# A list scheduler's model of TensorE in the input stage of a pooling and recurrence layer: waits for splits, x operands and a bank's last sum, and a rank penalty

## The chip, the cores and the metric

The kernel runs on one core of one Trainium2 chip. The metric is the device time of one execution in microseconds (us). The time of the kernel before is the median of three runs.

## The reference

One layer of a decoder, in fp32, for 2048 new tokens and 8 sequences of 8 tokens that go on from a state. Cut to what matters:

```python
xn = rms_norm(x, norm_pre)
z = einsum('btd,de->bte', xn, w_in)          # D 1024 -> 4096: v_pool, g_pool, u_lru, g_lru
y_pool = pool_mixer(v_pool, ...)             # windows 2/4/8/16 minus the token, a 256x256 map per group, a scale
xs = causal_conv(u_lru, ...)                 # depthwise, width 4
y_lru = rg_lru(xs, ...)                      # gates r, i = sigmoid(xs @ w + b), h = a*h + u along the tokens
mixed = concat([y_pool * silu(g_pool), y_lru * silu(g_lru)])
out = x + rms_norm(einsum('bte,ed->btd', mixed, w_out), norm_post)
```

The last rows of the pool and conv inputs and the recurrence's last state are outputs too.

## The kernel before

**Numbers and products.** TensorE multiplies fp32 operands that are split in two parts, a high one (rounded by ACT) and a low one (the rest, subtracted by DVE); three matmuls (high by high, high by low, low by high) stand for one. The input product z = xn @ w_in is tiled in three macros (m = 0, 1, 2) of 704 tokens each and in 16 quads of output channels, V (pool input), G (pool gate), U (recurrence input) and L (recurrence gate) by p = 0 to 3. In macro 0 a quad is eight plain half products. In macros 1 and 2 it is one level of Strassen-Winograd: seven products of 12 matmuls each, numbered 1 to 7 (`pid`), which are summed in three PSUM banks named a, e and d with macro and kind (a1G is bank a of a G quad in macro 1). Products 1, 6, 7 and 4 go through bank a, 5 and 3 through e, 2 through d. When a product is done, an evacuation copies the bank (ACT, L1011) or adds it to the result (DVE, L1007), and a later product of the same bank starts with what the earlier one left only after that evacuation has read it.

**Operands.** The x operands of the seven products are X11, X22, X21 and the sums T1 to T4 of quarters of x. They lie in one buffer, XN, that all quads of a macro share. At the change of macro, `transition` (L1340 to 1391) makes them anew: a raw sum on DVE (`x_raw`), the high part on ACT (`x_hi`, L334 and L336) and the low part on DVE (`x_lo`, L321). T2's sum needs T1's, T4's needs T2's. The weights' parts are loaded raw in macro 0 and for the last quads of macro 1, summed and split there (`w1V` from `wr1V`, `hi_lo` at L843), and stored in a DRAM scratch `wsd`, from where the other quads load them ready-made (`w2V<-wsd`, `w_step` at L897) six products ahead (AHEAD).

**Around the products.** Each finished quad starts a chain of work: the cumulative sums and differences of the pool and its map (six matmuls, bank y), the convolution and the two gates (six matmuls each, banks r and i, operands xh and xl), the gates' activations, the scan along the tokens, and SiLU. The row norms of the next macro are computed too (`tok_rsqrt`, L291 to 299: five small DVE operations with a square root on ACT between). After the input stage comes the output product, seven products by the same scheme with banks p.

**What sets the order.** Each engine runs its instructions in the order in which the program issues them. In the input stage that order is made in Python, on the host, by a list scheduler with a model of time: `T[0]` is the model's time, `clock` holds when DVE ("V"), ACT ("A") and GpSimd ("G") will be free. Each chain of work is a generator (a job) that yields the engine it needs next and for how long. `one_slot` (L1462) issues one product (`pe_fn`), then the evacuations of the product before (`run_evacs`, L1449), then at most one gate or map, and then fills the slot: `run_jobs` (L781) grants to jobs what can start before the slot's end, the earliest start first; among starts that are within 0.05 us of each other the lower rank wins. A slot lasts SLOT = 1.94 us and 0.98 for a gate or map, longer if the evacuations end later. Where a product needs something that is not issued yet, `need_w` (L910), `need_x` (L1393) and `need_small` (L954) issue it on the spot; the model's time does not move on for that. `quad_slot` (L1031) issues a product and hands its evacuation to the next slot. If no free buffer is left for the next quad, a later product may be issued ahead; this is how product 4 of a quad comes to stand behind products of the next one, or in front of them.

Of the kernel before, what the change touches and what calls it, by code (L numbers as in the profile page):

```python
# [52 lines left out]
LATE = 544  # L53
N_TT = (T_ALL + P - 1) // P
NBLK = 16
SLOT = 1.94
HOP = 0.2
OVER = 1.0
AHEAD = 6
# [14 lines left out]
def hymba_kernel(  # L74
# [392 lines left out]
    A = {}  # L467
# [268 lines left out]
    w_tiles, w_rawt = {}, {}  # L736
# [44 lines left out]
    def run_jobs(end):  # L781
        moved = True
        while moved:
            moved = False
            for job in list(jobs):
                while job in jobs:
                    e, arg = job["req"][:2]
                    if e == "?" and arg():
                        job["ready"] = max(job["ready"], T[0])
                    elif e == "t":  # L790
                        job["ready"] += arg
                    elif e == "D" and job["ready"] <= end:
                        pass
                    else:
                        break
                    advance(job)
            best = None
            for job in jobs:
                s = fits(job, end)
                if s is None:  # L800
                    continue
                req = job["req"]
                late = s + (TABLE_COST if len(req) > 2 and table[0] not in TABLES[req[2]] else 0.0)
                if best is None or late < best[0] - 0.05:
# [35 lines left out]
    def w_key(kind, p, pid):  # L840
        return wsd[:, (KINDS[kind] // 8 * NG + p) * 7 + pid - 1, :]

    def hi_lo(hi, lo, src, store=None):  # L843
        yield "A", 0.62
        AC.copy(out=hi, in_=src)
        yield "V", 0.71
        tsub(lo, src, hi.bitcast(F32))
        if store:
            yield "t", LAG
            yield "D", 0  # L850
            nc.sync.dma_start(out=w_key(*store[1:]), in_=store[0].bitcast(F32))
# [3 lines left out]
    def plain_tile(q, n):  # L855
        t = w_tiles[q, n] = half_tile(f"w{q[2]}{q[1]}_{n}")
        store = (flat_of(t), q[2], q[1], PLAIN_PID[n]) if n in PLAIN_PID else None
        w_jobs[q, n] = spawn(hi_lo(t[:, 0, :], t[:, 1, :], w_rawt[q, n], store), rank=0)

    def s_sum(q, i):  # L860
        r11, r12, r21, r22 = (w_rawt[q, n] for n in NAMES)
# [31 lines left out]
    def w_step(q, pid):  # L893
        m, p, kind = q
        t = w_tiles[q, pid] = half_tile(f"w{m}{kind}{p}_{pid}")
        if not is_late(q) or pid in (1, 2, 4):
            nc.sync.dma_start(out=flat_of(t).bitcast(F32), in_=w_key(kind, p, pid))  # L897
            return
        n = S_PID.index(pid)
        if n == 0:  # L900
            w_jobs[q, "s"] = {"n": 0, "job": spawn(s_sums(q, lambda i: w_jobs[q, "s"].update(n=i + 1)),
                                                        max(T[0], w_time[q]), rank=0)}
        box = w_jobs[q, "s"]

        def wait_split():
            yield "?", lambda: box["n"] > n
            yield from hi_lo(t[:, 0, :], t[:, 1, :], w_rawt[q, S_OF[pid]], (flat_of(t), kind, p, pid))
        w_jobs[q, pid] = spawn(wait_split(), rank=0)

    def need_w(q, n):  # L910
        if (q, "s") in w_jobs and w_jobs[q, "s"]["n"] < 4 and n in (5, 6, 7, 3):
            job = w_jobs[q, "s"]["job"]
            while w_jobs[q, "s"]["n"] <= S_PID.index(n):
                grant(job, max(clock["V"], job["ready"], T[0]))
        job = w_jobs.pop((q, n), None)
        if job:
            force(job)

    small = {}

# [10 lines left out]
    def load_small(m, kind, p):  # L931
        t = sb.tile([P, 2, 512], F32R, tag=kind, bufs=1, name=f"{kind}{m}_{p}")
        small[kind] = t
        flat = t.rearrange("p a b -> p (a b)").bitcast(F32)
        i = 0 if kind == "pw" else 1
        if m:
            nc.sync.dma_start(out=flat, in_=swd[:, i, p, :])
            return
        if (kind, p) not in small_raw:
            small_early(kind, p)  # L940
        r = small_raw.pop((kind, p))

        def work():
            yield "A", 0.62
            AC.copy(out=t[:, 0, :], in_=r)
            yield "V", 0.71
            tsub(t[:, 1, :], r, t[:, 0, :].bitcast(F32))
            t_done(1)
            yield "t", LAG
            yield "D", 0  # L950
            nc.sync.dma_start(out=swd[:, i, p, :], in_=flat)
        small[kind, "job"] = spawn(work(), rank=1)

    def need_small(kind):  # L954
        job = small.pop((kind, "job"), None)
        if job:
            force(job)

    Q = {}

# [72 lines left out]
    def quad_slot(q, pid):  # L1033
        t = Q[q]
        need_w(q, pid)
        w = w_tiles.pop((q, pid))
        key = {1: "a", 6: "a", 7: "a", 4: "a", 5: "e", 3: "e", 2: "d"}[pid]
        first = pid in (1, 5, 2)
        if first:
            t[key] = z_psum(f"{key}{q[0]}{q[2]}{q[1]}")[:, :CW]  # L1040
        z = t[key]
        need_x(XOF[pid], q[0])
        quad_product(z, w, XOF[pid], first, True, True)
        j, c, add = {1: (0, 0, 0), 5: (1, 1, 0), 6: (0, 1, 0), 3: (0, 1, 1), 7: (1, 1, 1), 2: (0, 0, 1), 4: (1, 0, 0)}[pid]

        def evac():
            (put_sum if add else put_copy)(q, j, c, z)
            if pid == 4:
                quad_end(q)
        return [("V", 0.52, evac) if add else ("A", 0.45, evac)]  # L1050
# [296 lines left out]
    def transition(m):  # L1347
# [46 lines left out]
    def need_x(n, m):  # L1394
        if "sums" not in x_jobs or m != x_macro[0]:
            return
        if n != "X11":
            while n not in x_jobs:
# [542 lines left out]
```

## Time and profile before

| | us |
|---|---|
| median of three runs | 1167.55 |
| lowest, highest run | 1165.06, 1172.33 |
| the profiled execution | 1172.25 |
| its span, first to last instruction | 1170.5 |
| TensorE busy in it | 1129.9 |
| DVE, ACT, GpSimd busy in it | 823.9, 651.1, 165.9 |
| mean granted clock of TensorE in it | 0.993 |

The times are device times. The profile shows one execution. Its rows are read so: a start in us, a length in us, the engine, the line, the operation, and what it writes and reads; in brackets the idle time of that engine just before, and the instruction or transfer that ended it. PE is TensorE, SP the engine that issues most of the transfers. In a table by stretches each engine's busy time is followed by its number of instructions, and then come the clock that TensorE was granted, the share of the 16 transfer engines that was busy, and GB/s.

### The profile page before, as it was taken

Reading aid. Unit: us, or ns where it says so; the run is one execution under the profiler, and the core shown is the slowest. Engines: PE = TensorE matmul, PEld = TensorE weight load, DVE = VectorE, ACT = ScalarE, POOL = GpSimd, SP = SyncE. Lnnn points to the kernel's source line nnn. Section 1 sums busy time; section 2 is a strip of 40 time slices with the busy share of each in tenths; the row PEclk is TensorE's granted clock in tenths of the full one; section 3 lists DMA queues with packets and bytes.
Section 4 is the critical chain, followed back from the end, with each engine's and each line's share of the span. In section 5 each row is a group of like instructions: output and inputs, shape, how many; then the busy total and the mean of one; then the engine's idle time right before and its main releaser. Section 6 shows DMA issues by size and latency. Waiting matters only on the chain. (4 is left out here: it accounts for less than half of the span.)

```text
span 1170.5 us, 17746 instructions
## 1 busy us (share of the span) xinstructions
PE 1129.9 (97%) x6274; PEld 1056.9 (90%) x6274; DVE 823.9 (70%) x1323; ACT 651.1 (56%) x1108; POOL 165.9 (14%) x264
## 2 busy tenths in 40 slices
PE   7999999999899999999799999999999999999996
PEld 6999999999899999999799999999888888888875
DVE  6797684868767757479658665646577668778777
ACT  5378675687548667568366726365864232335232
POOL 4201101001101200101013111201010003221332
PEclk9999999999999999999899999999999999999998
DMA  9665977985788889997799999998779677766563
GB/s 328 230 218 209 351 268 259 362 320 209 243 306 289 323 285 327 383 391 273 268 310 382 385 360 343 354 358 291 204 223 274 175 200 216 207 211 200 162 182 125
DMA packets 177464, 322.10 MB, mean 275 GB/s; under 512 B 24736, under 2 KB 86432, under 8 KB 177376
## 3 DMA queue, kind: packets, MB, share of 16 engines
q1 hardware_dynamic: 173536, 303.67, 75.8%
q0 software_dynamic: 3840, 17.30, 3.7%
q8 instruction: 49, 0.80, 0.3%
q14 instruction: 39, 0.32, 0.1%
HBM read 218.51 MB, written 102.15 MB: 274 GB/s over the span
## 5 line engine op out<-in xcount | busy, mean ns | idle before, releaser
L458 PE MATMUL p<-XN,s 128*128 128x512 f32 (+1 forms) x224 | 86.9, 388 | 1.4 <-DVE s L141 1.4
L456 PE MATMUL p<-XN,s 128*128 128x512 f32 (+1 forms) x224 | 86.8, 387 | 0.0
L457 PE MATMUL p<-XN,s 128*128 128x512 f32 (+1 forms) x224 | 86.8, 387 | 0.0
L1199 DVE SCALAR_TENSOR_TENSOR xs<-u,parT,xs 128x704 f32<-128x704 f32 (+1 forms) x72 | 67.8, 954 | 24.3 <-ACT xs L1188 23.8
L149 ACT ACT_TABLE_LOAD x65 | 83.4, 1283 | 1.9 <-PEq L1920 0.8
L449 POOL TENSOR_TENSOR xr<-ac,xr 128x512 f32<-128x512 f32 x27 | 50.8, 1902 | 213.8 <-DVE ac L590 104.4
L251 PE MATMUL zL<-XN,wL 128*128 128x352 f32 x384 | 64.5, 325 | 0.6 <-DVE wL L321 0.6
L1162 DVE SCALAR_TENSOR_TENSOR g<-y,parT,g 128x352 f32<-128x352 f32 x48 | 27.9, 581 | 52.3 <-PE y L251 52.3
L569 ACT ACTIVATE p<-ac 128x512 f32<-128x512 f32 (+1 forms) x32 | 18.8, 587 | 80.3 <-DVE ac L449 80.3
L251 PEld LDWEIGHTS zL<-XN,wL 128*128 128x128 f32 x384 | 62.6, 188 | 0.9 <-DVE wL L321 0.9
L1171 POOL DMA_DIRECT2D mixed<-g x24 | 13.2, 549 | 306.1 <-DVE g L1162 101.2
L138 ACT CAST s<-a 128x512 fp32r<-128x512 f32 x48 | 28.6, 616 | 48.5 <-DVE a L449 34.3
L449 DVE TENSOR_TENSOR a<-a,a 128x512 f32<-128x512 f32 x48 | 32.9, 689 | 31.0 <-DMA a<-mixed 27.6
L251 PE MATMUL y<-dh,pw 128*128 128x352 f32 x192 | 54.2, 324 | 0.4 <-DMA pw<-swd 0.4
L456 PE MATMUL p<-XN,a 128*128 128x512 f32 x137 | 54.2, 396 | 0.0
L458 PE MATMUL p<-XN,a 128*128 128x512 f32 x137 | 54.2, 396 | 0.0
L457 PE MATMUL p<-XN,a 128*128 128x512 f32 x137 | 54.2, 395 | 0.0
L458 PEld LDWEIGHTS p<-XN,s 128*128 128x128 f32 x224 | 42.1, 188 | 11.3 <-DVE s L141 1.8
L457 PEld LDWEIGHTS p<-XN,s 128*128 128x128 f32 x224 | 42.1, 188 | 9.5
L456 PEld LDWEIGHTS p<-XN,s 128*128 128x128 f32 x224 | 42.1, 188 | 9.4
L251 PE MATMUL zV<-XN,wV 128*128 128x352 f32 x288 | 48.5, 324 | 0.0
L251 PE MATMUL zU<-XN,wU 128*128 128x352 f32 x288 | 48.4, 324 | 0.0
(343 smaller groups left out, 3133.7 us busy)
## 6 DMA issues: line engine op xcount, KB each, us to landing
a<-mixed SPq DMA_DIRECT2D x112, 256.0 KB, 4.1
mixed<-g POOLq DMA_DIRECT2D x48, 352.0 KB, 6.3
w2V<-wsd SPq DMA_DIRECT2D x28, 512.0 KB, 7.7
w2G<-wsd SPq DMA_DIRECT2D x28, 512.0 KB, 7.2
w2U<-wsd SPq DMA_DIRECT2D x28, 512.0 KB, 7.5
w2L<-wsd SPq DMA_DIRECT2D x28, 512.0 KB, 7.0
wsd<-XN SPq DMA_DIRECT2D x27, 512.0 KB, 5.1
w1V<-wsd SPq DMA_DIRECT2D x24, 512.0 KB, 6.4
```

Source lines behind the costliest of these rows:

```text
L138: hi_eng.copy(out=hi, in_=src)
L149: nc.scalar.preload_act_table_set(name)
L251: nc.tensor.matmul(out, lhsT=lhsT, rhs=rhs, start=start, stop=stop)
L449: (eng or nc.vector).tensor_tensor(out=out, in0=a, in1=b, op=op)
L456: nc.tensor.matmul(out, lhsT=ah, rhs=wh, start=start and k == 0, stop=False)
L457: nc.tensor.matmul(out, lhsT=ah, rhs=wl, start=False, stop=False)
L458: nc.tensor.matmul(out, lhsT=al, rhs=wh, start=False, stop=stop and k == KT - 1)
L569: nc.scalar.activation(out=junk, in_=o, func=AF.Square, accum_out=st[:, g:g + 1])
L1162: V.scalar_tensor_tensor(out=g[:, cs], in0=Y, scalar=col(C_SCALE, blk), in1=g[:, cs], op0=ALU.mult, op1=ALU.mult)
L1171: nc.gpsimd.dma_start(out=mixed[:, blk, m * MW:(m + 1) * MW], in_=g[:, :MW])
L1199: V.scalar_tensor_tensor(out=xs, in0=E[:, k:k + n], scalar=col(C_CW + 8 * k, b), in1=xs, op0=ALU.mult, op1=ALU.add)
```

## The change

The change touches only the scheduler's model. The instructions that are issued, with their shapes and operands, stay the same; their order on the engines does not.

- SLOT goes from 1.94 to 1.93, and the length of a gate or map from 0.98 to GATE = 0.965.
- The model's TensorE now waits. `pe_after(at)` moves the start of the product that is being issued to `at`: for its weights' split (`w_fin`, filled by `hi_lo`), for its x operand (`x_fin`, filled by `put` in `transition`), for a gate's or map's weights (`need_small`), and, where the product is not its bank's first, for the bank's last evacuation (`t["f" + key]`). The slot then starts at that time.
- A late evacuation no longer makes the slot longer for everything: the end of the slot is its start and its length.
- In `run_jobs` the start that a job is compared by is later by 0, 0.2, 0.3 or 0.4 us for ranks 0 to 3 (`PENALTY`).

The diff, without the arguments that only pass a key on:

```diff
-SLOT = 1.94
+SLOT = 1.93
+GATE = 0.965
+PENALTY = (0.0, 0.2, 0.3, 0.4)
...
                 late = s + (TABLE_COST if len(req) > 2 and table[0] not in TABLES[req[2]] else 0.0)
+                late += PENALTY[job["rank"]]
                 if best is None or late < best[0] - 0.05:
...
+    w_fin, x_fin, pe_at = {}, {}, [0.0]
+
+    def pe_after(at):
+        pe_at[0] = max(pe_at[0], at)
...
         tsub(lo, src, hi.bitcast(F32))
+        if key:
+            w_fin[key] = clock["V"] + HOP
...
         if job:
             force(job)
+        pe_after(w_fin.get((q, n), 0.0))
...
+            w_fin[kind] = clock["V"] + HOP
...
+        pe_after(w_fin.get(kind, 0.0))
...
+        if not first:
+            pe_after(t["f" + key])
+
         def evac():
             (put_sum if add else put_copy)(q, j, c, z)
+            t["f" + key] = clock["V" if add else "A"] + HOP
...
             x_lo(n, src[n], {"V": V, "G": G}[eng])
+            x_fin[n] = clock["V"] + HOP
...
         force(x_jobs[n])
+        pe_after(x_fin[n])
...
         length = SLOT if pe_fn else 1.0
+        pe_at[0] = T[0]
         outs = pe_fn() if pe_fn else []
-        end = run_evacs(evacs)
+        run_evacs(evacs)
+        T[0] = pe_at[0]
         evacs[:] = outs
         for job in [j for j in jobs if j["req"][0] == "P"]:
             if job["ready"] <= T[0] + 0.3:
+                pe_at[0] = T[0] + length
                 evacs.extend(job["req"][1]())
-                length += 0.98
+                length = pe_at[0] - T[0] + GATE
...
-        end = max(T[0] + length, end + 0.1)
+        end = T[0] + length
         run_jobs(end)
```

How the order moves is shown at three places. In the changed file the helpers stand two lines lower: the splits and raw sums of L321 are at L323, the evacuations of L1007 at L1021.

**DVE at the first change of macro** (from macro 0 to 1). `XA<-XA` is a raw sum of x, `XN<-XA,XN` the low part of an operand, `e<-e1V` and the like the evacuations of the first V quad of macro 1. Before:

```order
L321 TENSOR_TENSOR XN<-XA,XN 128x1408
L321 TENSOR_TENSOR w1V_7_3117<-wr1V_21_2779,w1V_7_3117 128x512
L321 TENSOR_TENSOR XA<-XA 128x2x352 x2
L1007 TENSOR_TENSOR e_1_3123<-e1V_3145,e_1_3123 128x352
L321 TENSOR_TENSOR XN<-XA,XN 128x1408
L1007 TENSOR_TENSOR e_1_3123<-d1V_3203,e_1_3123 128x352
L324 TENSOR_TENSOR wr1G_22_2970<-wr1G_21_2968,wr1G_22_2970 128x512
L321 TENSOR_TENSOR w1G_5_3159<-wr1G_22_2970,w1G_5_3159 128x512
L1007 TENSOR_TENSOR e_1_3125<-a1V_3127,e_1_3125 128x352
L321 TENSOR_TENSOR XN<-XA,XN 128x1408
```

Now:

```order
L323 TENSOR_TENSOR XN<-XA,XN 128x1408 x3
L323 TENSOR_TENSOR wr1V_11_2788<-wr1V_22_2794,wr1V_11_2788 128x512
L323 TENSOR_TENSOR w1V_5_3049<-wr1V_22_2794,w1V_5_3049 128x512
L323 TENSOR_TENSOR wr1V_12_2790<-wr1V_12_2790,wr1V_11_2788 128x512
L323 TENSOR_TENSOR w1V_6_3070<-wr1V_11_2788,w1V_6_3070 128x512
L323 TENSOR_TENSOR w1V_7_3123<-wr1V_21_2792,w1V_7_3123 128x512
L323 TENSOR_TENSOR XN<-XA,XN 128x1408
L323 TENSOR_TENSOR w1V_3_3085<-wr1V_12_2790,w1V_3_3085 128x512
L326 TENSOR_TENSOR wr1G_22_2975<-wr1G_21_2973,wr1G_22_2975 128x512
L323 TENSOR_TENSOR wr1G_21_2973<-wr1G_11_2969,wr1G_21_2973 128x512
L323 TENSOR_TENSOR w1G_5_3166<-wr1G_22_2975,w1G_5_3166 128x512
L1021 TENSOR_TENSOR e_1_3127<-e1V_3152,e_1_3127 128x352
```

The last raw sums (not among these rows now) and the last split have moved ahead of the evacuation of e1V, and three splits stand in a row ahead of the weights 5, 6, 7 and 3. On TensorE, product 4 of this V quad is now issued behind products 1 and 5 of the G quad; it was ahead of them.

**DVE at the second change of macro** (from 1 to 2). `t_0` and `t_1` are the buffer of T2 and T4. Before:

```order
L1007 TENSOR_TENSOR e_2_5746<-e2V_5773,e_2_5746 128x288
L1007 TENSOR_TENSOR e_2_5746<-e2V_5773,e_2_5746 128x8x8
L321 TENSOR_TENSOR XA<-XA 128x2x352 x2
L321 TENSOR_TENSOR XN<-XA,XN 128x1408
L1007 TENSOR_TENSOR e_2_5746<-d2V_5846,e_2_5746 128x352
L1007 TENSOR_TENSOR e_2_5749<-a2V_5752,e_2_5749 128x288
L1007 TENSOR_TENSOR e_2_5749<-a2V_5752,e_2_5749 128x8x8
L321 TENSOR_TENSOR t_0_5706<-XA,t_0_5706 128x704
L321 TENSOR_TENSOR t_1_5707<-XA,t_1_5707 128x704
```

Now:

```order
L323 TENSOR_TENSOR XN<-XA,XN 128x1408
L1021 TENSOR_TENSOR g_1_5601<-a1L_5602,g_1_5601 128x352
L323 TENSOR_TENSOR XN<-XA,XN 128x1408 x2
L323 TENSOR_TENSOR XA<-XA 128x2x352 x2
L323 TENSOR_TENSOR XN<-t_0_5711,XN 128x704
L323 TENSOR_TENSOR XN<-t_1_5712,XN 128x704
L1292 SCALAR_TENSOR_TENSOR g_1_5260<-rg_4_5146,g_1_5260 128x704
L323 TENSOR_TENSOR t_0_5711<-XA,t_0_5711 128x704
L323 TENSOR_TENSOR t_1_5712<-XA,t_1_5712 128x704
L323 TENSOR_TENSOR XN<-XA,XN 128x1408
L1021 TENSOR_TENSOR e_2_5751<-e2V_5774,e_2_5751 128x288
L1021 TENSOR_TENSOR e_2_5751<-e2V_5774,e_2_5751 128x8x8
```

The raw sums of T3 (`XA<-XA`) and T4 (`t<-XA,t`) and T3's split stand ahead of the evacuation of e2V; they stood behind it. The first three splits of these rows are X22's, X21's and T1's; T1's was ahead of the other two before. On TensorE product 4 of the V quad is again issued two products later, behind products 1 and 5 of G.

**DVE at the third place**, late in macro 1: the evacuations of the last G quad and the small operations of the row norms (`tok`). Before:

```order
L1007 TENSOR_TENSOR g_1_5053<-d1G_5193,g_1_5053 128x352
L1095 TENSOR_REDUCE s_1_5244<-e_1_4923 128x1
L1097 SCALAR_TENSOR_TENSOR s_1_5244<-e_1_4923,s_1_5244 128x703
L1007 TENSOR_TENSOR g_1_5054<-a1G_5055,g_1_5054 128x352
L321 TENSOR_TENSOR w1L_7_5263<-wr1L_21_5080,w1L_7_5263 128x512
L293 TENSOR_SCALAR tok<-tok 128x6
L296 RECIPROCAL tok<-tok 128x6
```

Now:

```order
L1021 TENSOR_TENSOR g_1_5057<-d1G_5197,g_1_5057 128x352
L1113 TENSOR_REDUCE s_1_5248<-e_1_4914 128x1
L1115 SCALAR_TENSOR_TENSOR s_1_5248<-e_1_4914,s_1_5248 128x703
L295 TENSOR_SCALAR tok<-tok 128x6
L298 RECIPROCAL tok<-tok 128x6
L299 TENSOR_TENSOR tok<-tok 128x6
L300 SCALAR_TENSOR_TENSOR tok<-tok 128x6
L301 SCALAR_TENSOR_TENSOR tok<-tok 128x6
L1021 TENSOR_TENSOR g_1_5058<-a1G_5059,g_1_5058 128x352
```

The five small operations have moved from behind the evacuation of a1G to ahead of it.

Elsewhere most gates and maps, and the DVE and ACT work around them, change places by a slot or two. On TensorE the first gate r of macro 0, which stood behind two half products of the second V quad and a map between them, is now issued ahead of all three.

More of the change, by code (lines that the diff above doesn't have):

```diff
@@ L841, in w_key, with hi_lo @@
         return wsd[:, (KINDS[kind] // 8 * NG + p) * 7 + pid - 1, :]
-    def hi_lo(hi, lo, src, store=None):
+    w_fin, x_fin, pe_at = {}, {}, [0.0]
+    def pe_after(at):
+        pe_at[0] = max(pe_at[0], at)
+    def hi_lo(hi, lo, src, store=None, key=None):
         yield "A", 0.62
@@ L857, in plain_tile @@
         store = (flat_of(t), q[2], q[1], PLAIN_PID[n]) if n in PLAIN_PID else None
-        w_jobs[q, n] = spawn(hi_lo(t[:, 0, :], t[:, 1, :], w_rawt[q, n], store), rank=0)
+        w_jobs[q, n] = spawn(hi_lo(t[:, 0, :], t[:, 1, :], w_rawt[q, n], store, (q, n)), rank=0)
     def s_sum(q, i):
@@ L906, in wait_split @@
             yield "?", lambda: box["n"] > n
-            yield from hi_lo(t[:, 0, :], t[:, 1, :], w_rawt[q, S_OF[pid]], (flat_of(t), kind, p, pid))
+            yield from hi_lo(t[:, 0, :], t[:, 1, :], w_rawt[q, S_OF[pid]], (flat_of(t), kind, p, pid),
+                             (q, pid))
         w_jobs[q, pid] = spawn(wait_split(), rank=0)
```

## The prediction

> **What bounds the kernel now.** I read the page first, then TensorE's waits, then a table by stretches, then the timelines of PE, DVE and ACT around the longest waits. The page:
>
> ```profile
> span 1170.5 us, 17746 instructions
> PE 1129.9 (97%) x6274; PEld 1056.9 (90%) x6274; DVE 823.9 (70%) x1323; ACT 651.1 (56%) x1108; POOL 165.9 (14%) x264
> ```
>
> TensorE is busy 97% of the span, and the change neither adds nor removes a matmul. So all that it can win is idle time of TensorE and time at a lower clock; all that it can lose is new idle time. The waits of PE, those on loads and one on a bank's sum, and the table by stretches (busy time of PE, PEld, DVE, ACT and POOL, granted PE clock, DMA share, GB/s):
>
> ```profile
> PE a2L L249 <- DMA w2L<-wsd: 3.1, 2, 2.0
> PE a2V L249 <- DMA w2V<-wsd: 2.1, 3, 1.4
> PE a2G L249 <- DMA w2G<-wsd: 1.7, 1, 1.7
> PE a1V L249 <- DVE e L1007: 0.6, 1, 0.6
> ...
> 64.00:296.00 232.00, 232.00 (x1435) 232.00 (x1436) 171.27 (x253) 168.20 (x270) 18.13 (x46) 1.00 0.77 281
> 544.00:592.00 48.00, 40.75 (x227) 39.44 (x226) 32.59 (x40) 18.08 (x28) 7.70 (x16) 0.93 0.83 292
> 592.00:784.00 192.00, 186.53 (x1140) 184.90 (x1140) 124.97 (x196) 109.06 (x176) 29.55 (x64) 1.00 0.97 359
> ```
>
> From 64 to 296 us TensorE does not idle at all: nothing to win there, only to lose. The first change of macro (near 300) and the second (near 570) are where it idles for the input splits; from 592 on it idles 5.5 us, mostly for loads. Both stretches with a clock below 1.00 are such idle places. How the clock goes down is seen in windows of 3.41 us:
>
> ```profile
> 307.46:310.87 3.41, 1.61 (x9) 1.11 (x7) 2.72 (x5) 0.62 (x1) 0.00 (x0) 1.00 0.33 125
> 310.87:314.28 3.41, 3.28 (x11) 3.28 (x12) 3.38 (x6) 0.00 (x0) 0.00 (x0) 0.50 0.95 265
> ...
> 720.47:723.88 3.41, 1.63 (x11) 1.34 (x9) 0.82 (x2) 3.36 (x5) 0.00 (x0) 1.00 1.04 422
> 723.88:727.29 3.41, 3.23 (x20) 3.26 (x21) 0.53 (x1) 1.33 (x2) 0.00 (x0) 1.00 1.02 390
> ```
>
> A window with 1.80 us of idle PE (3.41 less 1.61) was followed by a window at clock 0.50; one with 1.78 us was not. In the slow window 11 matmuls ran instead of some 21. So a stall of about 1.8 us inside such a window costs itself and 1.7 us more (below, 11 matmuls take 3.52 us, where 12 at full clock take 1.96 from start to start).
>
> **The first change of macro.** PE's timeline, then DVE's:
>
> ```profile
> 294.97 2.12 PE L249 MATMUL a1V<-XN,w1V 128*128 128x352 f32 x12
> ...
> 300.41 2.05 PE L249 MATMUL a1V<-XN,w1V 128*128 128x352 f32 x11 [1.20 <-DVE XN L321]
> ...
> 309.52 0.40 PE L249 MATMUL a1V<-XN,w1V 128*128 128x352 f32 x1 [0.84 <-issue]
> 311.00 3.52 PE L249 MATMUL a1V<-XN,w1V 128*128 128x352 f32 x11 [1.09 <-DVE XN L321]
> 314.35 1.96 PE L249 MATMUL a1G<-XN,w1G 128*128 128x352 f32 x11
> ```
>
> ```profile
> 300.88 1.69 DVE L321 TENSOR_TENSOR XA<-XA 128x704 f32<-128x704 f32 x2
> 304.52 0.53 DVE L1007 TENSOR_TENSOR e<-e1V,e 128x352 f32<-128x352 f32 x1 [1.95 <-PE e1V L249]
> ...
> 309.33 1.61 DVE L321 TENSOR_TENSOR XN<-XA,XN 128x1408 fp32r<-128x1408 f32 x1
> ```
>
> From a1V at 294.97 to a1G at 314.35 seven products take 19.38 us; at 1.96 each they need 13.72. The loss is 5.66 us. DVE stands 1.95 us behind a sum of bank e1V that TensorE has not finished, while the last operand (T4) still waits to be split; T4's lower half is made at 309.33 and PE waits for it. The order of the change has all splits ahead of that sum, and product 4, which uses T4, two products later (3.92 us). The 1.61 us of the last split then lie in the 1.95 us gap, and the waits at 300.41 and 311.00 go, with the slow window. What becomes late next: three operand splits in a row (1.6 us each) stand ahead of the lower halves of weights 5 and 3, which I count at 0.4 and 0.3 us. Loss after 0.7, so **−4.9** (bounds: 0, if the wait goes to the weights; −5.7, if all goes).
>
> **The second change of macro.** PE, then DVE:
>
> ```profile
> 553.61 2.12 PE L249 MATMUL a2V<-XN,w2V 128*128 128x352 f32 x12
> ...
> 561.07 2.18 PE L249 MATMUL a2V<-XN,w2V 128*128 128x352 f32 x12 [1.43 <-DMA w2V<-wsd]
> ...
> 568.95 0.43 PE L249 MATMUL a2V<-XN,w2V 128*128 128x352 f32 x1 [1.80 <-ACT XN L336]
> 570.61 3.42 PE L249 MATMUL a2V<-XN,w2V 128*128 128x352 f32 x11 [1.23 <-DVE XN L321]
> 576.31 0.43 PE L249 MATMUL a2V<-XN,w2V 128*128 128x352 f32 x1 [2.29 <-ACT XN L334]
> 577.24 3.51 PE L249 MATMUL a2V<-XN,w2V 128*128 128x352 f32 x11 [0.50 <-DVE XN L321]
> 580.59 1.61 PE L249 MATMUL a2G<-XN,w2G 128*128 128x352 f32 x9
> ```
>
> ```profile
> 554.25 3.15 DVE L321 TENSOR_TENSOR XN<-XA,XN 128x1408 fp32r<-128x1408 f32 x2
> ...
> 565.31 0.59 DVE L1007 TENSOR_TENSOR e<-e2V,e 128x288 f32<-128x288 f32 x2 [3.70 <-PE e2V L249]
> ...
> 568.93 1.62 DVE L321 TENSOR_TENSOR XN<-XA,XN 128x1408 fp32r<-128x1408 f32 x1 [1.43 <-ACT XN L336]
> ...
> 574.57 1.68 DVE L321 TENSOR_TENSOR t<-XA,t 128x704 f32<-128x704 f32 x2
> ```
>
> Eight products take 580.59 − 553.61 = 26.98 us; at 1.96 they need 15.68; 11.3 us are lost, among them two slow windows. DVE waits 3.70 us for the bank e2V with the raw sums of T3 behind it, then for the next bank with those of T4 behind it (574.57). In the new order both raw sums and T3's split are ahead of the e2V sum, and product 4 comes after two products of G. But the lower half of T1 now comes after the copies of X22 and X21: a1L's sum ends at about 554.5 by its rows' lengths, then two splits of 1.57 us each (3.15 for two) end near 557.7, where the second product would read it at about 555.7. That is a new wait of 2.0 us, and it covers the 1.43 of the load at 561.07, which lands at the same time as before. With 0.2 for small ones the loss after is 2.2: **−9.1** (bounds: −11.3; or only the half, −5.6, if the loads of w2V take the place of the splits; a slow window after the new wait would cost 1.7).
>
> **The third place, near 510.**
>
> ```profile
> 510.63 2.21 PE L249 MATMUL a1G<-XN,w1G 128*128 128x352 f32 x12 [1.31 <-DVE g L1007]
> ```
>
> ```profile
> 510.08 0.50 DVE L1007 TENSOR_TENSOR g<-a1G,g 128x352 f32<-128x352 f32 x1
> ...
> 511.09 0.17 DVE L293 TENSOR_SCALAR tok<-tok 128x6 f32<-128x6 f32 x1
> ...
> 512.21 0.17 DVE L299 SCALAR_TENSOR_TENSOR tok<-tok 128x6 f32<-128x6 f32 x1
> ```
>
> ```profile
> 507.78 1.28 ACT L149 ACT_TABLE_LOAD   x1
> ```
>
> Product 4 of G writes the bank a1G, so it waits for that sum. The five small operations on the row norms (with a square root on ACT between them) took from 511.09 to 512.38, 1.29 us, behind the sum; the change puts them ahead of it. The wait grows from 1.31 to 2.6, over the 1.8 at which a window was slow: +1.3 and +1.7, **+3.0** (bounds: 0, if DVE comes to this place earlier than now; +4.3, if the table load of the square root, now done well ahead, falls among the five).
>
> **Smaller terms.** The 0.6 at a1V<-e goes, since product 4 now leaves its bank two products more: **−0.6**. The first gate is issued two half products and a map earlier, where the second V quad begins:
>
> ```profile
> 79.26 2.12 PE L251 MATMUL zV<-XN,wV 128*128 128x352 f32 x12
> ...
> 80.19 0.78 ACT L1204 CAST xh<-xs 128x704 fp32r<-128x704 f32 x1 [3.15 <-DVE xs L1199]
> ...
> 81.40 0.88 DVE L321 TENSOR_TENSOR xl<-xs,xh 128x704 fp32r<-128x704 f32 x1
> ```
>
> It then stands at 79.26 and needs xh and xl, which ended at 80.97 and 82.28; the new order brings both about two short DVE operations forward, to some 80.3 for xl. Wait **+1.0** (0, if xl is brought forward by 2.1; 3.0, if it ends at 82.28 as now). The many other gates and products that change places by one or two I cannot follow one by one; the stretch 64 to 296 has no idle time to give, so I take **+1.0** for them (−1 to +4). The loads: 544 to 592 moves 0.83 × 48 = 39.8 us of transfers, and the highest share of the table is 1.04, so they need 38.3 us; with 9.1 us fewer the stretch has 38.9. It just fits, and some backlog meets the saturated 592 to 784. I add one more wait of a2G's size, **+1.7** (0 to 9.1).
>
> Sum: −4.9 − 9.1 − 0.6 + 3.0 + 1.0 + 1.0 + 1.7 = −7.9 us. The profiled execution took 1172.25 (span 1170.5 and 1.75 around it), which becomes 1164.35. That execution is 4.7 above the median of the runs, 1167.55; the same difference from the median gives **1159.7 us**. The planner's constants (1.94 to 1.93, 0.98 to 0.965, penalties of 0.2 to 0.4 for ranks) cost nothing themselves: they run on the host, and act only through the order counted above.
>
> **Rivals.** A: the sum above. B: the new order is clean. 510 is reached with DVE ahead, loads take nothing back, nothing else is new: −4.9 − 9.1 − 0.6 + 1.0 = −13.6, 1153.9. For it: most of DVE's work has slack (70% busy). Against: 510 lies in a stretch where DVE follows late loads. C: the loads set the pace of the last macro and take all 9.1 of the second change back instead of 1.7: −0.5, 1167.0. For it: share 0.97 over 192 us and three kinds of load that PE already waits for. Against: 359 GB/s on average where 422 were reached in one window. The Trainium skill, "DMA: Bandwidth & Descriptors", section "Where 436 GB/s comes from", gives about 358 GB/s as a core's share of the memory, which would make C certain; the window at 422 disagrees with it as a ceiling here. D, the slower side: as C, but TensorE, arriving 9.1 us early, gives them back in five stalls of 1.8 us or more between 592 and 784, each followed by a slow window: 8.5 more, so +8.0, 1175.6. It decides from 1.8 us a stall on; the three longest waits on loads now are 2.0, 1.7 and 1.4, near that edge. E: the change does not do what it says at the changes of macro: the splits come early, but DVE's queue hands the wait to weights and T1, and half of the 14.0 stays: −0.9, 1166.6. F: the wait of 2.6 at 510 does not slow the clock: −9.6, 1157.9. It would be so if the 2.6 fall across two windows with less than 1.8 in each. The Trainium skill, "TensorE: Matmul & The Clock Gate", section "HAM oscillation — how this bites in real kernels", has it that idle gaps must exceed about 3.4 us for that; by that rule F holds. The trace disagrees: 1.80 us sufficed at 307.46.
>
> **Chances.** A 0.42, B 0.16, C 0.15, D 0.07, E 0.08, F 0.12. The range goes from 1152 (B with one stall less) to 1170 (C and E with their own spread); D lies outside, with the far ends of B. A change of 1% is 11.7 us, about what these runs (1165.06 to 1172.33) can tell from none: faster than 1155.9 is most of B and a part of A and F, 0.22; slower than 1179.2 only the worst of D, 0.04; between, 0.74.
>
> **What would show it.** In the changed profile: eight products of the second change of macro in 18 us with no clock of 0.50 there, and a wait of about 2 us of the second product for DVE's XN; seven of the first in about 14.4; near 500 to 510 a wait of a1G for DVE's g of 2 to 3 us and a slow window behind it; a first gate that waits about 1 us near 75 to 80; waits on w2 loads that sum to 7 or 8 us. The prediction is wrong if TensorE's idle time in the input stage does not fall by some 5 us, if the 64 to 296 stretch shows idle time of more than 5, or if loads take all of the second gain.

## The result, and the profile after

| | before | changed |
|---|---|---|
| median of 6 runs, us | 1169.34 | 1159.38 |
| lowest, highest | 1165.06, 1172.33 | 1156.17, 1161.36 |
| span of the profiled execution | 1170.5 | 1157.6 |
| TensorE's granted clock in it | 0.993 | 0.995 |

The ratio is 0.9917, 95% interval 0.9893 to 0.9941: 10 us less at the medians. With three more runs the median of the kernel before is 1169.34, where the prediction started from 1167.55. The two profiled executions lie 12.9 us apart in their spans; the rest of that is told below. One of the four executions of the kernel both_moves below took 1566.4 us at a granted clock of 0.657, and no comparison uses it.

First the page and TensorE's waits in the changed kernel (what waited for what: us in total, times, longest). The four instructions that ACT has more are table loads, 69 where there were 65; the counts of the other engines on this page are the same.

```profile
span 1157.6 us, 17742 instructions
PE 1127.9 (97%) x6274; PEld 1056.3 (91%) x6274; DVE 826.7 (71%) x1323; ACT 656.0 (57%) x1112; POOL 160.4 (14%) x264
```

```profile
PE e2G L251 <- ACT g L1025: 3.6, 2, 3.1
PE a1G L251 <- DVE g L1021: 2.7, 1, 2.7
PE e2V L251 <- DVE XN L323: 1.7, 1, 1.7
...
PE a2L L251 <- DMA w2L<-wsd: 0.8, 2, 0.5
...
PE r L253 <- DVE xl L323: 0.7, 1, 0.7
```

The waits for XN of the two changes of macro are gone but for one, at e2V. Three stand at the top: e2G behind ACT, which is new and which the prediction had not priced, a1G behind DVE, the place near 510, which was 1.3, and e2V, which is new too. The loads, which were the longest waits of the last macro, are at 0.8 us and less. By stretches (PE, PEld, DVE, ACT, POOL busy, PE clock, DMA share, GB/s):

```profile
64.00:296.00 232.00, 231.31 (x1428) 231.02 (x1429) 172.32 (x255) 170.47 (x270) 19.71 (x47) 1.00 0.76 278
...
544.00:592.00 48.00, 43.15 (x255) 42.56 (x254) 37.66 (x50) 22.95 (x37) 10.41 (x18) 0.96 0.94 329
592.00:784.00 192.00, 189.19 (x1153) 186.90 (x1152) 121.51 (x193) 114.87 (x178) 24.57 (x62) 1.00 0.98 360
```

The transfers of the second change now fill the stretch (0.94 where it was 0.83), and the last macro still has less idle time, not more: 2.8 us where there were 5.5.

The two changes of macro on TensorE, the first:

```profile
296.09 2.12 PE L251 MATMUL a1V<-XN,w1V 128*128 128x352 f32 x12
...
306.23 2.11 PE L251 MATMUL a1V<-XN,w1V 128*128 128x352 f32 x12
308.18 2.11 PE L251 MATMUL a1G<-XN,w1G 128*128 128x352 f32 x12
```

and the second:

```profile
551.04 2.12 PE L251 MATMUL a2V<-XN,w2V 128*128 128x352 f32 x12
...
555.04 2.05 PE L251 MATMUL e2V<-XN,w2V 128*128 128x352 f32 x11 [1.71 <-DVE XN L323]
...
564.77 2.12 PE L251 MATMUL a2V<-XN,w2V 128*128 128x352 f32 x12
566.73 2.12 PE L251 MATMUL a2G<-XN,w2G 128*128 128x352 f32 x12
...
570.65 2.12 PE L251 MATMUL a2V<-XN,w2V 128*128 128x352 f32 x12
```

At the first change the six products of V ahead of G run from 296.09 to 308.18, 12.09 us, without a bracket: 0.3 more than at 1.96 each, where 0.7 was expected. At the second the eight products from 551.04 take 17.7 us, where 18 were expected; the only stall is that of T1's low part, 1.71 us, and no run of matmuls is stretched by a slow clock; product 4, at 570.65, finds its operand ready.

The losses: near 510 (TensorE, then DVE),

```profile
506.56 3.68 PE L251 MATMUL a1G<-XN,w1G 128*128 128x352 f32 x12 [2.67 <-DVE g L1021]
```

```profile
504.80 0.15 DVE L295 TENSOR_SCALAR tok<-tok 128x6 f32<-128x6 f32 x1
...
505.91 0.17 DVE L301 SCALAR_TENSOR_TENSOR tok<-tok 128x6 f32<-128x6 f32 x1
505.99 0.52 DVE L1021 TENSOR_TENSOR g<-a1G,g 128x352 f32<-128x352 f32 x1
```

and behind the second change (TensorE; ACT; the queue of SP, which issues the load):

```profile
577.86 3.37 PE L251 MATMUL e2G<-XN,w2G 128*128 128x352 f32 x12 [3.14 <-ACT g L1025]
```

```profile
576.84 0.62 ACT L1463 CAST XA<-wb 128x512 fp32r<-128x512 f32 x1 [7.50 <-DMA wb<-in_w_out]
577.37 0.45 ACT L1025 COPY g<-e2G 128x352 f32<-128x352 f32 x1
```

```profile
567.29 0.43 SPq L391 DMA_DIRECT2D wb<-in_w_out  x1
```

ACT's queue holds the first split of an output weight (`region_chain`, for the output stage, not urgent) ahead of the evacuation of e2G. Its load, issued at 567.29, landed 9.5 us later; the model allows 3.0. ACT stood 7.5 us, TensorE 3.14 of them, and the 12 matmuls behind ran at the low clock (3.37 us, where 12 take 2.12 at full clock).

Since both programs have the same 6274 matmuls, the start of TensorE's k-th matmul in one profile less that in another is a running account. For the changed kernel less the kernel before, and for the experiments less the kernel before (us, negative is earlier; single gates that stand elsewhere in the order make 1 us of noise, and each row is one execution, where executions of one kernel lie up to 5 us apart, 1156.17 to 1161.36 for the changed one):

| k (place) | 1700 (first gates) | 1860 (first change) | 2990 (before 510) | 3060 (after it) | 3280 | 3390 (second change) | 3450 (after e2G) | 3780 | 4500 (end of input) |
|---|---|---|---|---|---|---|---|---|---|
| changed | 1.1 | −3.9 | −5.4 | −2.7 | −2.6 | −11.9 | −7.0 | −5.4 | −9.2 |
| tok_behind | 1.8 | −3.2 | −5.0 | −5.0 | −4.6 | −14.0 | −10.1 | −8.8 | −13.5 |
| wout_split_later | 0.9 | −4.5 | −6.4 | −4.1 | −3.9 | −13.3 | −13.4 | −10.3 | −14.6 |
| both_moves | 0.4 | −4.9 | −5.6 | −5.6 | −5.2 | −14.5 | −14.5 | −12.0 | −14.4 |
| both_moves_two_op | 0.4 | −5.0 | −5.7 | −5.8 | −5.4 | −14.7 | −14.7 | −14.1 | −20.7 |
| splits_late | 0.5 | −1.6 | −3.4 | −1.1 | −0.9 | −5.4 | −5.5 | −4.1 | −7.8 |
| product4_early | 2.2 | 2.3 | 5.8 | 5.7 | 10.6 | 9.9 | 10.0 | 12.2 | 7.7 |
| numbers_alone | 0.1 | −5.6 | 0.3 | 2.1 | 2.3 | −7.1 | −7.2 | −6.1 | −9.1 |
| waits_alone | 1.6 | −3.2 | −2.5 | −3.0 | −2.5 | −8.5 | −2.9 | 0.7 | −1.1 |
| no_tensor_waits | 3.1 | 3.5 | 12.1 | 11.6 | 15.3 | 16.4 | 16.3 | 17.8 | 11.8 |
| no_bank_wait | 0.5 | −4.4 | −6.2 | −6.1 | −5.9 | −15.2 | −11.5 | −10.1 | −13.2 |
| no_penalty | 0.9 | 0.8 | 1.7 | 3.6 | 3.7 | −5.7 | −4.0 | −1.7 | −3.5 |
| old_slot | 1.6 | 0.0 | −1.3 | −1.8 | −1.1 | −8.5 | −7.1 | −0.7 | −0.4 |

At the end of the input stage the changed kernel is 9.2 us ahead. The profiled execution of before then lost 1.6 us more in the output stage, 1.4 of them at a wait for s on DVE, and had a tail after the last matmul that was 2.1 us longer. The order there is nearly the same in both, so I put these 3.7 us down to the one execution, not to the change; that is argued, not shown. The medians (10.0 us) fit the 9.2.

### The profile page after: what moved, and what is told of

It is laid out like the page before. It is cut to its first block, busy times and chain, and to the rows that moved or that the text cites. A ratio compares the mean times of both kernels' runs of the same rounds, so it can differ in the third digit from the quotient of the medians.

```text
span 1157.6 us, 17742 instructions
## 1 busy us (share of the span) xinstructions
PE 1127.9 (97%) x6274; PEld 1056.3 (91%) x6274; DVE 826.7 (71%) x1323; ACT 656.0 (57%) x1112; POOL 160.4 (14%) x264
## 5 line engine op out<-in xcount | busy, mean ns | idle before, releaser
L253 PE MATMUL zG<-XN,wG 128*128 128x352 f32 x288 | 47.9, 325 | 0.0
```

Source lines behind the costliest of these rows:

```text
L253: nc.tensor.matmul(out, lhsT=lhsT, rhs=rhs, start=start, stop=stop)
```

## The experiments

The theory on trial: the gain is made by the order at the two changes of macro (splits ahead of the sums, product 4 behind two products of G), and given back in part at two places where something not urgent stands ahead of an evacuation. Its rivals: the loads of the last macro set the pace, so that what is won early is lost late; or the waits in the scheduler's model are themselves what is needed.

**The two losses, one move each.** A list holds an emission back until so many evacuations have been issued; the model's clocks are not touched, so that nothing else moves.

```diff
# tok_behind
-        tok_rsqrt(tiles[0], tiles[-1] + 1)
+        later.append([1 if m == LM else 0, lambda: tok_rsqrt(tiles[0], tiles[-1] + 1)])
# wout_split_later: n is 6 for the first output weight, else 0
-            AC.copy(out=region(r, k, 0), in_=src)
+            later.append([n, lambda k=k, src=src: AC.copy(out=region(r, k, 0), in_=src)])
...
# both, in run_evacs, after each evacuation
             fn()
+            run_later(1)
```

> Only the five row-norm operations of the third place go back behind the evacuation of a1G; nothing else moves. If they are the cost at that place, the wait of a1G for DVE falls from 2.67 us to about 1.4, the slow window behind it goes (12 matmuls in about 1.96 instead of 3.48 us), and the time falls by 2.8 us against the change: about 1156.6. The rival, that the loads of the last macro set the pace anyway, expects the same stall to go but the 2.8 us to come back as waits on w2 loads after 592 us: about 1159.4.

Measured: 0.9875 of before (0.986 to 0.9891), median 1154.35. TensorE at the place:

```profile
505.77 2.22 PE L251 MATMUL a1G<-XN,w1G 128*128 128x352 f32 x12 [1.45 <-DVE g L1021]
507.82 2.12 PE L251 MATMUL a1L<-XN,w1L 128*128 128x352 f32 x12
```

The stall is 1.45 and the slow window is gone: in the account this kernel passes 510 without a change (−5.0 to −5.0) where the changed kernel loses 2.7. The five small operations were the cost there. The waits compare cleanly: in both kernels TensorE was ready for this product 8.8 us after DVE's work behind the load of wr1L had started, and the wait differs by 1.22 us, about what the five operations take (1.28). The whole gain against the changed kernel is larger, 4.3 us at the end of the input stage: the stall at e2G was shorter too (−14.0 to −10.1 is 3.9, against 4.9), since the load of wb was used 8.6 us after its issue, not 9.5, and the rest lies in the last macro. Neither is shown to come from the move.

> Only the first split of an output weight (ACT's cast of wb and DVE's subtraction) is issued later, behind the evacuations of G's first products in the last macro. If ACT's queue, held by that cast until its load lands, is what e2G waits for, the wait of 3.14 us and the slow window behind it go: 4.7 us less than the change, about 1154.7. The rival that loads set the pace expects new waits on w2 loads of the same size: about 1159.4.

Measured: 0.9886 (0.9872 to 0.9901), median 1156.32. TensorE:

```profile
573.10 2.11 PE L251 MATMUL e2G<-XN,w2G 128*128 128x352 f32 x12
...
619.91 2.18 PE L251 MATMUL a2V<-XN,w2V 128*128 128x352 f32 x12 [1.96 <-DMA w2V<-wsd]
```

At e2G no wait is left (−13.3 to −13.4, where the changed kernel goes from −11.9 to −7.0): 4.9 us, as thought. But a load is now late at 619.91, by 1.96. By the ratios the gain against the changed kernel is 3.6 us, not 4.7, but the two intervals overlap, so that the times alone do not tell 3.6 from 4.7.

> Both single moves together. If the two stalls are independent, 2.8 and 4.7 add: 7.5 us less than the change, about 1151.9, and 17 to 18 us less than before. If loads set the pace, not below 1157.

Measured: 0.988 (0.9861 to 0.99), no better than either alone. The two stalls are both gone, and the account stands at −14.5 behind e2G; then −12.0, and −14.4 at the end, a gain of 2.4, where the changed kernel gains 3.8 us over the same last stretch. What took it, on TensorE, on SP's queue, and on GpSimd:

```profile
710.02 3.69 PE L251 MATMUL a2L<-XN,w2L 128*128 128x352 f32 x12 [2.10 <-DMA w2L<-wsd]
```

```profile
690.28 0.98 SPq L907 DMA_DIRECT2D w2L<-wsd  x2
698.87 0.34 SPq L1108 DMA_DIRECT2D out<-op  x1
699.30 0.38 SPq L907 DMA_DIRECT2D w2L<-wsd  x1
```

```profile
697.34 0.61 POOL L1106 COPY op<-e 128x15 f32<-128x15 f32 x1 [20.66 <-DMA out<-op]
```

This looks like the rival: a gain given back to a late load. The rows tell of another cause. SP issued nothing for 7.6 us, from 691.3 to 698.9, because the store `out<-op` at the head of its queue waited for GpSimd's copy into op, and that copy waited for the first store of the same buffer to land. The loads of w2L stood behind it. Of op there is one buffer.

```diff
-                op = sb.tile([P, N_S + 1, PB], F32, tag="op", bufs=1, name=f"op{blk}")
+                op = sb.tile([P, N_S + 1, PB], F32, tag="op", bufs=2, name=f"op{blk}")
```

> The kernel with both single moves, with two buffers instead of one for the small tile op that holds a pool quad's last rows; no instruction changes its place. In the kernel with both moves GpSimd's second copy into op waits until the first has been stored, SP's queue stands behind the second store (8.2 us from 691 to 699), and the w2L loads queued behind it land late: TensorE waits 2.1 us for one at 710 and a slow window follows, 3.3 us together. If it is SP's blocked queue that gives the time back, that wait and window go, and the time falls to about 1152, 3 less than with both moves. If it is the transfers' rate in the last macro, the wait stays: 1155.

Measured: 0.9837 (0.9817 to 0.9857), median 1148.8, the fastest of all: 5.0 us under both_moves by the ratios, 6.3 by the medians (1155.14 there) and in the account. SP's queue at the same place, and TensorE's longest waits:

```profile
687.67 0.97 SPq L907 DMA_DIRECT2D w2L<-wsd  x2
689.55 0.34 SPq L1108 DMA_DIRECT2D out<-op  x1
690.83 0.32 SPq L907 DMA_DIRECT2D w2L<-wsd  x1
```

```profile
PE e2V L251 <- DVE XN L323: 1.7, 1, 1.7
PE a1G L251 <- DVE g L1021: 1.5, 1, 1.5
PE i L253 <- ACT rg L1248: 0.9, 1, 0.9
```

The second store is issued 1.9 us after the loads, not 8.6, and the load behind it at 690.83. No w2 load is left among the waits above 0.5 us: from 592 to 784 TensorE is busy for 191.5 of 192 us, where it was 187.6, while the busy share of the transfers rises from 0.97 to 0.99. So the pace of the last macro was not set by the transfers' rate; the late loads came from a queue that stood behind one small store. The expectation of 3 us was about half of the gain: I had counted the one stall at 710, but the four V quads of the last macro all store through op.

**Where the gain comes from: the splits or product 4.** In splits_late the operands T3 and T4 are held back to their old places; TensorE's order is untouched.

```diff
+    HOLD = {(0, "T3"): ((1, 0, "V"), 3), (0, "T4"): ((1, 0, "V"), 7), (1, "T3"): ((2, 0, "V"), 3), (1, "T4"): ((2, 0, "V"), 7)}
...
-            x_lo(n, src[n], {"V": V, "G": G}[eng])
+            hold(m, n, False, lambda: x_lo(n, src[n], {"V": V, "G": G}[eng]))
...
             t["f" + key] = clock["V" if add else "A"] + HOP
+            release((q, pid))
```

> The changed kernel, with the operands T3 and T4 put back to where they stood before: at the first change of macro their low parts behind the sums of e1V and a1V, at the second T3 behind the sum of e2V and T4 behind that of a2V. TensorE's order stays, with product 4 two products later. If the place of the splits is what won the time, the second change shows waits for XN again, about 2.0 and 1.3 us at product 7 with a slow window and some 2 at product 4; the first about 0.8 at product 7. The wait of e2G for ACT goes in return, since TensorE comes later than the load. Sum +0.8 +5.1 +2.0 -4.7, so about 1162.6. If the later place of product 4 alone won the time, no wait for XN comes back: 1159.4.

Measured: 0.9931 (0.9906 to 0.9956), median 1161.45. TensorE at the first change, at the second, and DVE there:

```profile
308.32 2.05 PE L251 MATMUL a1V<-XN,w1V 128*128 128x352 f32 x11 [2.43 <-DVE XN L323]
...
568.39 0.43 PE L251 MATMUL a2V<-XN,w2V 128*128 128x352 f32 x1 [1.79 <-ACT XN L338]
570.05 3.33 PE L251 MATMUL a2V<-XN,w2V 128*128 128x352 f32 x11 [1.23 <-DVE XN L323]
...
577.11 2.11 PE L251 MATMUL a2V<-XN,w2V 128*128 128x352 f32 x12
```

```profile
564.75 0.59 DVE L1021 TENSOR_TENSOR e<-e2V,e 128x288 f32<-128x288 f32 x2 [5.69 <-PE e2V L251]
565.26 1.68 DVE L323 TENSOR_TENSOR XA<-XA 128x704 f32<-128x704 f32 x2
```

Product 7 waits as it did before the change, 1.79 and 1.23 with a slow window, and the chain is the same: T3's raw sum behind the sum of e2V. Product 4, at 577.11, does not wait: its late place alone covers T4. Of 9.3 us at the second change 4.5 remain (−0.9 to −5.4). The wait of e2G is gone, which is why the total hardly suffers: the load of wb, issued at 573.79, was used 4.5 us later, at 578.25, and TensorE came to that product at 581.00. The wait at the first change was 2.43, three times what I thought.

```diff
# product4_early
+        for l in lasts[:2]:
+            k = slots.index(next(s_ for s_ in slots if s_[2:] == (QUADS[l + 1], 4)))
+            p = [s_[2:] for s_ in slots[k - 2:k + 1]]
+            for d, s_ in enumerate([p[2], p[0], p[1]]):
+                slots[k - 2 + d] = slots[k - 2 + d][:2] + s_
```

> The changed kernel with product 4 of the first V quad of macros 1 and 2 issued where it stood before, ahead of the two G products. The splits of T3 stay early. If both the splits' place and that of product 4 count at the second change, product 4 waits there for T4, 1 to 2.5 us, and products 5 to 7 for nothing but T1; at the first change it waits some 0.8 us for a1V's sum. The row norms fall behind a1G's sum in this order, which saves 2.8. About 1160. If the split alone counted, no wait for XN at product 4.

Measured: 1.0036 (1.0014 to 1.0058), median 1175.36. A miss: the order shifted in many other places with it. At its own place TensorE shows

```profile
313.10 3.38 PE L251 MATMUL a1V<-XN,w1V 128*128 128x352 f32 x12 [3.71 <-DVE e L1021]
...
586.07 3.26 PE L251 MATMUL a2V<-XN,w2V 128*128 128x352 f32 x12 [3.75 <-DMA w2V<-wsd]
```

No wait for XN, but one of 3.71 for its bank's sum and one of 3.75 for its own weight, each with a slow window. At the second change this kernel gains next to nothing (10.6 to 9.9). So both halves count: the early splits of T3 serve product 7, as splits_late shows, and the late place of product 4 covers its operand, its bank and its load. For the late place the evidence is these two rows alone; with so much else moved, the total of this kernel tests nothing.

**Which part of the change makes that order.** Two kernels with a part of the change alone, and four with a part taken away.

```diff
# numbers_alone: the kernel before, with
-SLOT = 1.94
+SLOT = 1.93
+PENALTY = (0.0, 0.2, 0.3, 0.4)
...
+                late += PENALTY[job["rank"]]
...
-                length += 0.98
+                length += 0.965
# no_penalty, and waits_alone: the changed kernel, with
-PENALTY = (0.0, 0.2, 0.3, 0.4)
+PENALTY = (0.0, 0.0, 0.0, 0.0)
# old_slot, and waits_alone too
-SLOT = 1.93
-GATE = 0.965
+SLOT = 1.94
+GATE = 0.98
# no_bank_wait, and no_tensor_waits
-        if not first:
-            pe_after(t["f" + key])
# no_tensor_waits too
-        pe_after(w_fin.get((q, n), 0.0))
...
-        pe_after(w_fin.get(kind, 0.0))
...
-        pe_after(x_fin[n])
```

> The kernel before with only the constants: a slot of 1.93, a gate of 0.965 and the rank penalties; TensorE in the model does not wait, and a late evacuation still stretches its slot. In its order the splits of T3 and T4 stand ahead of the sums of e1V and e2V and product 4 is late at both changes, as in the changed kernel, and the row norms stand ahead of a1G's sum, the first output weight ahead of e2G's. If the order at these places is all that counts, about 1160 (-10 against before). If the model's waits are needed for the gain, about 1169.

> The changed kernel with the old constants: slot 1.94, gate 0.98, no penalties; the waits and the slot without stretch stay. In its order the splits stand ahead of e1V's and e2V's sums, product 4 is late only at the second change, the row norms stand behind a1G's sum, and the first output weight still ahead of e2G's. -4 at the first change, -9.6 at the second, 0 near 510, +4.9 at e2G: about 1160, give or take the loads' 2. If the constants carry the gain: 1169.

> The changed kernel without the waits of TensorE in the model (weights, x operands, banks), with the new constants and without the stretch. In its order the first change of macro has the splits ahead of e1V's sum, but T3 stands behind e2V's sum and product 4 is early at both changes; the row norms stand behind a1G's sum and the output weight behind e2G's. If the order at these places counts: -4 at the first change, little at the second, nothing lost near 510 and at e2G: about 1164. If the waits in the model do not matter: 1159.

> The changed kernel without one of the waits in the model, that of a product for its bank's last evacuation. Its order differs from the changed kernel's in a handful of DVE, ACT and transfer rows, none of them at the places that were costed. So 1159.4, within 2. If holding up only the bank that is late were what the gain rests on, it would go back towards 1169.

> The changed kernel with the rank penalties at zero. The second change of macro, the place near 510 and that of the output weight have the changed kernel's order; at the first change the split of T4 falls behind e1V's sum and product 4 is early again. So some 2 to 4 of the 4.9 us at the first change come back and the rest stays: about 1162. If the penalties carry the gain: 1169.

> The changed kernel with the old slot (1.94 and 0.98) and the penalties and waits left in. T3's splits stand ahead of e1V's and e2V's sums, product 4 is late at the second change but early at the first, the row norms stand ahead of a1G's sum, and two output weights instead of one stand in ACT's queue around e2G's sum: about 1163, with the wait of e2G the largest. If the two constants carry the gain: 1169.

| kernel | ratio to before (95%) | median, us |
|---|---|---|
| changed | 0.9917 (0.9893 to 0.9941) | 1159.38 |
| numbers_alone | 0.9912 (0.9885 to 0.9939) | 1156.66 |
| waits_alone | 0.9986 (0.9971 to 1.0) | 1166.06 |
| no_tensor_waits | 1.0134 (1.011 to 1.0159) | 1184.57 |
| no_bank_wait | 0.9884 (0.9859 to 0.9909) | 1156.93 |
| no_penalty | 0.9956 (0.994 to 0.9973) | 1165.53 |
| old_slot | 0.9989 (0.9975 to 1.0002) | 1168.94 |

The constants alone, in the kernel before, give the whole gain; the waits alone give nothing that can be told from zero; and the changed kernel without its waits is slower than before. One pair narrows this down. numbers_alone and no_tensor_waits have the same constants and no waits; all that differs is that a late evacuation still makes the slot longer in the first. With that stretch the ratio is 0.9912, without it 1.0134. So in these orders the gain needed the new constants and one of the two things that hold the model back, the old stretch or the new waits. The slot without the penalties, and the penalties without the slot, were not tried with the old stretch. What each kernel makes is another order, and the account shows that the second change is won in most of them (−9.4 in numbers_alone, −6.0 in waits_alone, −9.4 in no_penalty, −7.4 in old_slot, −9.3 in no_bank_wait), but not in no_tensor_waits (+1.1), where T3 stands behind e2V's sum, as expected. The totals differ by what else the order hit. TensorE in numbers_alone, then waits of waits_alone, no_tensor_waits and old_slot, one fence each:

```profile
374.02 2.67 PE L250 MATMUL a1G<-XN,w1G 128*128 128x352 f32 x12 [2.95 <-DVE g L1009]
```

```profile
PE e2G L251 <- ACT g L1025: 3.9, 1, 3.9
PE a2V L251 <- DMA w2V<-wsd: 3.8, 4, 2.7
```

```profile
PE a1G L251 <- ACT g L1023: 3.6, 2, 3.5
PE e2V L251 <- DVE XN L323: 3.5, 1, 3.5
PE r L253 <- ACT xh L1217: 3.3, 1, 3.3
```

```profile
PE a2V L251 <- DMA w2V<-wsd: 3.7, 4, 1.9
PE e2U L251 <- ACT u L1025: 3.3, 1, 3.3
PE e2V L251 <- DVE XN L323: 2.5, 1, 2.5
```

Apart from the start, waits_alone, no_tensor_waits and old_slot have three or four stalls of 2 to 4 us each, at places of their own; numbers_alone has one of 2.95. My expectations for these kernels, made from the four places I had costed, were near for numbers_alone (1160 against 1156.7, with the stall at 374 and none at e2G, so in part by luck) and no_bank_wait (1159.4 against 1156.9), and too low for no_tensor_waits by 20 us, for old_slot and waits_alone by 6, for no_penalty by 3.5. The wait for a bank's last sum, by which late sums were to hold up only their own bank, has no share in the gain: without it the time is not longer. no_bank_wait also shows how much of the loss near 510 hangs on a load. The five operations stand ahead of a1G's sum there too, and yet that wait is 1.65 us with no slow window behind it (−6.2 to −6.1 in the account), not 2.67: DVE had stood there until the load of wr1L landed, and it went on at 493.26, not at 495.09, which is 1.0 us earlier against TensorE.

## Why the prediction was right

The forecast was 7.9 us less; measured are 10.0 at the medians and 9.2 in the account at the end of the input stage. By its terms:

| term | predicted | account |
|---|---|---|
| first change of macro | −4.9 | −5.0 (1.1 to −3.9) |
| second change of macro | −9.1 | −9.3 (−2.6 to −11.9) |
| a1V<-e and what lies between | −0.6 | −1.5 (−3.9 to −5.4) |
| near 510 | +3.0 | +2.7 (+0.1 in no_bank_wait) |
| first gate | +1.0 | +1.1 |
| not followed one by one | +1.0 | +4.9 (e2G) |
| loads of the last macro | +1.7 | −2.2 (−7.0 to −9.2) |

The two large terms rest on the right mechanism, shown by splits_late and product4_early: the old order brings the old waits back, with the same releasers. The chain by hand for T1's low part gave 2.0 us; it was 1.71. The stall near 510 was taken as 2.6 and was 2.67, and it did slow the clock, so rival F falls, and tok_behind shows the five operations as the cause of 1.2 us of it. That the sum came out so near is luck in part: the 2.67 lay in one window of 3.41 us (503.42 to 506.84), which the prediction could not know, and with the same order the wait was 1.65 in no_bank_wait, near the bound of 0 that the prediction gave for an earlier DVE.

Two terms were wrong, by +3.9 and −3.9 us, and cancelled; that is luck. It is luck too that the forecast time, 1159.7, lies 0.3 us from the median of 1159.38: the gain was 2 us larger than forecast, and the kernel before 1.8 us slower than its first three runs. The stall at e2G was not seen: the order showed the cast of wb ahead of e2G's evacuation, but I did not read ACT's queue there, nor ask what its load would take once TensorE came 9 us earlier into transfers that are dense. It is a wait on a load through another engine's queue, and wout_split_later shows it. The loads of the last macro were given the wrong sign. The step that failed is that TensorE's earlier arrival meets a saturated stretch and must wait for backlog. The share did rise to 0.94 and 0.98, but the waits on w2 loads came to 1.6 us, where 6.9 were before and 7 or 8 were expected; and both_moves_two_op leaves one of 0.5 at a share of 0.99. Rivals C and D, for which the transfers' rate is the limit, are refuted by that run. Why the changed kernel had fewer of these waits than the kernel before, with the same single buffer, was not tried by itself.

Rival E (half of the gain goes to weights and T1) did not happen. Rival B has its number reached by other means: with the two losses taken out one by one the kernels stand at 1154 to 1156, where B had 1153.9.

The reason I gave for the constants, that they act only through the order, holds. But nothing in the prediction told that the constants would do in the kernel before, or that without the waits and the stretch they would cost 15.6 us (by the ratio).

## What to carry to other kernels

A list scheduler's constants and its waits are judged by the order they make, not by whether the model is truer: print the order and read, at each place where the busiest engine can wait, what stands ahead of the releasing instruction on its engine. Work that is not urgent and that waits for a load must not stand ahead of an evacuation in an in-order queue, and a store from a single buffer must not stand ahead of loads. When two removed stalls do not add up, look in the queue of the wait that appeared before blaming bandwidth; a second buffer of 540 bytes per partition (9 by 15 fp32) was worth 5 to 6.3 us here.

## What the runs showed of the hardware

A stall of TensorE of about 2 us or more may cost itself alone or 1.2 to 1.6 us more, and its length does not decide. The stalls of 2.10 (710.02 in both_moves, 12 matmuls in 3.69), 2.67 (506.56 in the changed kernel, 3.68) and 3.71 (313.10 in product4_early, 3.38) were followed by slow matmuls; those of 2.43 (308.32 in splits_late, 11 in 2.05) and 1.96 (619.91 in wout_split_later, 12 in 2.18) were not.

The granted clock in the 14 traces tells what decides. In each trace every stretch at half clock begins a whole number of times 3.413 us after the first record at full clock (86, 162 and 164 times in the kernel before, 143 and 164 in the changed one). If each trace is cut into windows on this grid, from 64 us to 5 us before the last matmul ends, all 25 stretches at half clock follow a window in which TensorE was idle for 1.80 to 3.12 us. Of the windows at full clock with less idle time none was followed by such a stretch, and of those with 1.80 or more only one was not, with 1.83 (569.59 in no_tensor_waits). So the idle share of a window on a fixed grid counts, a little over half, and not the gap: the 2.43 left 1.62 us in its fullest window, the 1.96 about 1.3. The idle time rests on modelled ends of matmuls, and no run moved the windows by design. The Trainium skill ("TensorE: Matmul & The Clock Gate", section "HAM oscillation — how this bites in real kernels") asks for gaps of more than about 3.4 us; the 2.10 and 2.67 disagree.

A load of 256 KB (wb) that took a median of 3.6 us over the changed kernel took 9.5 where the transfers were dense (share 0.94); the scheduler allows 3.0 for it, and TensorE stood 3.14 behind it.
